# Hymba-style encoder step: order of the first loads, PSUM banks and engine of the token preparation, and the place of the per-layer input transposes

## Chip, core and metric

The kernel runs on one core of one Trainium2 chip, as one program. The metric is the device time of one execution in microseconds (us). A profile of one execution goes with it; its span runs from the first to the last instruction on the core.

## The reference

One layer of a streaming encoder is applied to 2048 prompt tokens and 32 sample tokens of width 1024, all in float32. The part that matters here, shortened:

```python
a  = rmsnorm(x, g_attn)                        # token preparation
z  = a @ w_in                                  # 3072 columns
qa, ka, va, qb, kb, vb = split(z)              # group A: 4 heads, group B: 8 heads
oa = diff_attn(qa, ka, va, t5_bias, lam)       # group A, all earlier keys
ob = band_attn(qb, kb, vb, clip_bias)          # group B, a band of 9 chunks of 64
h  = x + concat(norm(oa), norm(ob)) @ w_out
h  = h + square(relu(rmsnorm(h, g_mlp) @ w_up)) @ w_down
h  = h + sigmoid(h @ w_ple_gate) * (p @ w_ple_proj)   # p: per-layer inputs, 256 wide
y  = rmsnorm(h, g_final)
```

The sample tokens also attend to a cache of 128 keys and values. New keys and values are outputs too.

## The kernel before

Tokens are handled in four blocks (0 to 3) of 512; block 3 also has the 32 sample tokens. Float32 products are made of three matmuls (`mm3`, L164 to L170): each operand is split into a high part in float32r and a low part, and high x high, high x low and low x high are summed in a PSUM bank. `split` (L146) makes the two parts: the high one with a copy on ScalarE (ACT) or VectorE (DVE), the low one with a subtraction on GpSimd (POOL) or VectorE.

The stages that the change touches or displaces, in the order of the source:

1. `consts` (L191) makes the identity and loads four norm weights (`g_attn_s`, `g_mlp_s`, `g_b_s`, `g_sub_s`).
2. `prep` (L297) for blocks 0 and 1: each tile of 128 tokens is loaded (`x`), its mean square is taken on ScalarE (L306), it is transposed on TensorE (PE; `rp`, `xp`), scaled by VectorE (L323) into `a32`, and split into `aH` (VectorE) and `aL` (GpSimd). The transposes use the three banks of the pool `ps_s`.
3. `proj` (L336), group A, blocks 0 and 1: v (`vps`), q and k (`qps`), written to scratch in DRAM (`vS`, `qS`, `kS`). The high and low parts of q and k go through two buffers each, tags `qh` and `ql`.
4. `lam`, `biases` (L227) and `prep_p` (L753). `prep_p` loads the per-layer inputs (`pn`, two buffers), transposes them on TensorE into the pool `ps_t` (`ppt`, tag `tp`, two banks), makes a high part on ScalarE (`pph`, L773) and a low part on VectorE (`ppl`, L774) in the buffers `qh` and `ql`, and stores them in DRAM (`pS`), from where `gate` reads them much later.
5. Attention of group A for queries 0 to 1023 (`attn_a`, matmuls `s`, `tpp`, `o`).
6. Group B projections of blocks 0 to 2, with `prep` of blocks 2 and 3 woven in.
7. Attention of group B for queries 0 to 1023 (`attn_b`, 8 heads with 4 pairs of query tiles each). Per pair: scores `sb` (L704) into `ps_s`, bias and maximum on VectorE (L707), exponential and scaling on ScalarE (L712, L714), transposes `tpb` (L719) into `ps_t` (tag `tp`, the same two banks as `ppt`), high part on ScalarE (`pHb`, L728), low part on VectorE (`pLb`, L729), output `ob` (L744), sum of its halves (L749, L750).
8. `caches` (L446), which transposes the key caches and uses the buffers `qh` and `ql` too; then the group B projection of block 3, the rest of group B's attention, and the group A projections of blocks 2 and 3.
9. Output projection, MLP (`ups`, `dps`) and gate of blocks 0 and 1 around the rest of group A's attention, and then the same for blocks 2 and 3 without attention.

The framework's scheduler, not the source, fixes the order of instructions on each engine: it goes by priorities that follow the source's order, by its own estimate of durations, and by the availability of tile buffers. Buffers of a tag are handed out among its tiles one after another. So projections of a later stage are laid between the attention's instructions on TensorE where the buffers allow it. On each engine, instructions then run in the order written. All loads and stores are issued by SyncE (SP), in order.

Of the kernel before, what the change touches and what calls it, by code (L numbers as in the profile page):

```python
# [44 lines left out]
def toks(b):  # L45
    out = []
    for i in range(4):
        out.append((i * P, P))
    if b == 3:
        out.append((512, SS))  # L50
    return out
# [30 lines left out]
def drain(gen):  # L82
    for _ in gen:
        pass
# [48 lines left out]
class Kern:  # L133
# [57 lines left out]
    def consts(self, cp):  # L191
        nc, a = self.nc, self.a
        self.ident = cp.tile([P, P], F32, name="ident")
        make_identity(nc, self.ident)
        ones = cp.tile([P, P], F32, name="ones")
        nc.gpsimd.memset(ones, 1.0)
        self.ones = cp.tile([P, P], F32R, name="ones_r")
        nc.vector.tensor_copy(self.ones, ones)

        def cols(name, ap, k):  # L200
            t = cp.tile([P, k], F32, name=name)
            self.dma(t, ap.rearrange("(k p) -> p k", p=P))
            return t

        self.g_attn = cols("g_attn_s", a["g_attn"][0], 8)
        self.g_mlp = cols("g_mlp_s", a["g_mlp"][0], 8)
        self.g_b = cols("g_b_s", a["out_norm_b"][0], 4)
        self.g_sub = cols("g_sub_s", a["subln_g"][0], 1)
        nc.vector.tensor_scalar(self.g_sub, self.g_sub, 1.0 - LAM_INIT, None, op0=ALU.mult)
# [84 lines left out]
    def actpair(self):  # L294
        return [self.act.tile([P, 8, BLK], F32R, tag="act", name=n) for n in ("aH", "aL")]

    def prep(self, b, acts, pp, mm, tag):  # L297
        nc = self.nc
        aH, aL = acts[b]
        for c0, n in toks(b):  # L300
            t0 = 512 * b + c0
            x = pp.tile([P, D], F32, tag="x", name="x")
            self.dma(x[:n], self.xsrc(t0, n))
            a32 = pp.tile([P, 8, P], F32, tag="a32", name="a32")
            st = pp.tile([P, 1], F32, tag="st", name="st")
            nc.scalar.activation(  # L306
                a32[:n].rearrange("p a b -> p (a b)"), x[:n], AF.Square, accum_out=st[:n]
            )
            r = self.rsqrt(pp, st[:n], 1, 1.0 / D, EPS, nc.vector, "r1", n)
            rp = mm.tile([P, 512], F32, tag=tag, name="rp")  # L310
            nc.tensor.transpose(rp[:, :n], r.broadcast_to([n, P]), self.ident[:n, :n])
            rb = pp.tile([P, P], F32, tag="rb", name="rb")
            nc.scalar.activation(rb[:, :n], rp[:, :n], AF.Copy)
            xt = pp.tile([P, 8, P], F32, tag="xt", name="xt")
            for h in range(2):
                xp = mm.tile([P, 4, P], F32, tag=tag, name="xp")
                for k in range(4):
                    kk = 4 * h + k
                    nc.tensor.transpose(xp[:, k, :n], x[:n, kk * P : kk * P + P], self.ident[:n, :n])
                nc.scalar.activation(xt[:, 4 * h : 4 * h + 4, :n], xp[:, :, :n], AF.Copy)  # L320
                for k in range(4):
                    kk = 4 * h + k
                    nc.vector.scalar_tensor_tensor(  # L323
                        a32[:, kk, :n], xp[:, k, :n], self.g_attn[:, kk : kk + 1], rb[:, :n],
                        op0=ALU.mult, op1=ALU.mult,
                    )
            self.dma(self.xT[:, :, t0 : t0 + n], xt[:, :, :n])
            self.split(aH[:, :, c0 : c0 + n], aL[:, :, c0 : c0 + n], a32[:, :, :n], "dve", "pool")
            yield

    def ktok(self, b):
# [742 lines left out]
    def run(self):  # L1074
        tc, nc, a = self.tc, self.nc, self.a
        with ExitStack() as top:

            def opened(stack, name, bufs, space=None, side="left"):
                kw = {} if space is None else {"space": space}
                return stack.enter_context(  # L1080
                    tc.tile_pool(name=name, bufs=bufs, side=side, reuse_waits="tile", **kw)
                )

            nc.scalar.preload_act_table_set("natural_log_exp_and_others")
            cp = opened(top, "cp", 1)
            self.dp = opened(top, "dp", 1, bass.MemoryType.DRAM)
            self.wp = opened(top, "wp", 3)
            mm = opened(top, "mm", MM, PSUM)
            tp = mm
            psx = ExitStack()  # L1090
            ps_s = opened(psx, "pss", 5 - MM, PSUM, "right")
            ps_t = opened(psx, "pst", 2, PSUM, "right")
# [4 lines left out]
            sg = opened(s12, "sg", 2)  # L1097
            self.consts(cp)
            with ExitStack() as x:
                pp = opened(x, "pp0", 3, side="right")  # L1100
                acts = {b: self.actpair() for b in HALVES[0]}
                for b in HALVES[0]:
                    drain(self.prep(b, acts, pp, ps_s, "s"))
            ppx = ExitStack()
            pp = opened(ppx, "pp", 1)
            drain(self.proj(HALVES[0], 0, acts, sg, mm, Rings((ps_t, "tp"))))
            with ExitStack() as x:
                wk = opened(x, "setup", 1, side="right")
                self.lam(cp, wk)
                self.biases(wk, ps_t)  # L1110
                self.prep_p(sg, wk, ps_t)
            self.small = True
            mark = tc.tile_snap_priority()
            with ExitStack() as x:
                pool = opened(x, "a0", 1, side="right")
# [19 lines left out]
            weave(self.proj((2,), 1, acts, sg, mm, tp), lifted(self.prep(3, acts, pp, mm, "mm")), 3)  # L1135
            ppx.close()
            self.caches(sg, tp)
            drain(self.proj((3,), 1, acts, sg, mm, tp))
            wqx = ExitStack()
            wq = opened(wqx, "wq", 1, side="right")  # L1140
# [17 lines left out]
            with ExitStack() as x:  # L1158
                pool = opened(x, "a1", 1, side="right")
                for js in JA1:  # L1160
                    self.attn_a(js, pool, ps_s, ps_t, ps_o)
            wk = opened(sq_, "wk", 1)
# [41 lines left out]
            wk = opened(top, "wk4", 1)  # L1204
# [3 lines left out]
            act = Sized(opened(top, "acth", 4), BLK, True)  # L1208
# [75 lines left out]
```

## Time and profile before

| | |
|---|---|
| median of 3 runs | 3315.77 us (3314.72 to 3323.53) |
| the profiled execution | 3310.69 us |
| its span | 3308.8 us |
| granted TensorE clock, mean | 0.975 |
| DVE / ACT / POOL busy | 50% / 51% / 44% |

The page's second part cuts the span into 40 slices. TensorE is busy 90% or more of most of them, with 60% in the first, 80% and more in the third, fourth and some later ones. TensorE busy time is the union of its matmuls, whose ends are modelled, so a share of 90% has little left in it. Times in the views of the trace count from the start of the span.

### The profile page before, as it was taken

To read this page: it belongs to the slowest core of one execution; us is meant where nothing else is said; L and a number is where in the kernel's file an instruction comes from. 1 tells how busy PE (TensorE), PEld (TensorE's weight loads), DVE (VectorE), ACT (ScalarE), POOL (GpSimd) and SP (SyncE) were. 2 spreads that over 40 slices of the span, in tenths; PEclk is the share of its full clock that TensorE was granted. 3 is DMA by queue.
4 is the path that set the end of the run, shared out by engine and by line. 5 is a ranking of instruction groups with operands and counts; after the bars stand their busy time and mean duration, and the time that the engine had idled before them with its cause. 6 is when DMAs were issued, how large, how long until landed. Compare 5 with 4: busy or idle time off the path is not lost. (4 is left out here: it accounts for less than half of the span.)

```text
span 3308.8 us, 50118 instructions
## 1 busy us (share of the span) xinstructions
PE 3096.1 (94%) x17881; PEld 2710.5 (82%) x17881; DVE 1669.4 (50%) x3952; ACT 1698.4 (51%) x3717; POOL 1468.8 (44%) x1083
## 2 busy tenths in 40 slices
PE   6988989999989999999899999989889999999998
PEld 6877778889977888777777877877779999999987
DVE  6117777454555545476765656656442232223335
ACT  4226666566665766666665656654442222222245
POOL 4335654432334433444544444565753333333365
PEclk9999899999999999999999999999999999999999
DMA  7488777686788654545655345347631111111123
GB/s 232 159 252 244 205 217 205 204 247 195 215 235 215 180 145 134 155 132 138 200 136 136 112 132 144 116 146 226 178 105 52 45 46 50 46 45 45 53 86 101
DMA packets 519073, 488.93 MB, mean 148 GB/s; under 512 B 37884, under 2 KB 414016, under 8 KB 518824
## 3 DMA queue, kind: packets, MB, share of 16 engines
q1 hardware_dynamic: 518824, 485.73, 50.8%
q8 instruction: 142, 2.33, 0.3%
q14 instruction: 107, 0.88, 0.1%
HBM read 379.06 MB, written 110.49 MB: 148 GB/s over the span
## 5 line engine op out<-in xcount | busy, mean ns | idle before, releaser
L153 POOL TENSOR_TENSOR wl<-wr,wh 128x1024 fp32r<-128x1024 f32 x338 | 820.0, 2427 | 1026.3 <-ACT wh L149 983.4
L949 DVE TENSOR_TENSOR h<-h,dps 128x512 f32<-128x512 f32 (+1 forms) x640 | 373.1, 585 | 584.6 <-PE dps L170 572.2
L149 ACT ACTIVATE wh<-wr 128x1024 fp32r<-128x1024 f32 x338 | 356.9, 1056 | 563.9 <-PE dps L169 278.4
L168 PE MATMUL dps<-uh,wh 128*128 128x512 f32 (+1 forms) x1280 | 459.7, 359 | 22.0 <-DVE h L949 16.7
L168 PE MATMUL ups<-cH,wh 128*128 128x512 f32 (+1 forms) x1280 | 452.0, 353 | 8.2 <-ACT relu L914 8.0
L170 PE MATMUL dps<-uh,wl 128*128 128x512 f32 (+1 forms) x1280 | 451.7, 353 | 0.0
L169 PE MATMUL ups<-cL,wh 128*128 128x512 f32 (+1 forms) x1280 | 451.5, 353 | 0.0
L169 PE MATMUL dps<-ul,wh 128*128 128x512 f32 (+1 forms) x1280 | 451.4, 353 | 0.0
L170 PE MATMUL ups<-cH,wl 128*128 128x512 f32 (+1 forms) x1280 | 451.0, 352 | 0.0
L168 PEld LDWEIGHTS dps<-uh,wh 128*128 128x128 f32 x1280 | 242.8, 190 | 57.0 <-DVE h L949 22.8
L168 PEld LDWEIGHTS ups<-cH,wh 128*128 128x128 f32 x1280 | 241.4, 189 | 40.9 <-ACT relu L914 8.6
L170 PEld LDWEIGHTS dps<-uh,wl 128*128 128x128 f32 x1280 | 241.7, 189 | 33.0
L169 PEld LDWEIGHTS ups<-cL,wh 128*128 128x128 f32 x1280 | 241.9, 189 | 31.1 <-DVE cL L153 0.4
L170 PEld LDWEIGHTS ups<-cH,wl 128*128 128x128 f32 x1280 | 241.7, 189 | 30.1
L153 POOL TENSOR_TENSOR ul<-relu,uh 128x272 fp32r<-128x272 f32 (+1 forms) x160 | 174.9, 1093 | 205.2 <-ACT uh L149 203.8
L169 PEld LDWEIGHTS dps<-ul,wh 128*128 128x128 f32 x1280 | 242.4, 189 | 26.3
L168 PE MATMUL qps<-aH,wh 128*128 128x512 f32 (+1 forms) x640 | 231.5, 362 | 6.8 <-ACT wh L149 3.4
L545 PE MATMUL s<-ka,q 128*128 128x256 f32 (+4 forms) x784 | 192.7, 348 | 40.8 <-issue 15.7
L169 PE MATMUL qps<-aL,wh 128*128 128x512 f32 (+1 forms) x640 | 229.8, 359 | 0.0
L170 PE MATMUL qps<-aH,wl 128*128 128x512 f32 (+1 forms) x640 | 229.3, 358 | 0.0
L559 ACT ACTIVATE e<-s,nm 128x512 f32<-128x512 f32 (+3 forms) x256 | 155.1, 610 | 94.7 <-DVE nm L551 70.9
L545 PEld LDWEIGHTS s<-ka,q 128*128 128x128 f32 (+1 forms) x784 | 135.7, 195 | 66.4 <-issue 27.9
(217 smaller groups left out, 7056.9 us busy)
## 6 DMA issues: line engine op xcount, KB each, us to landing
wr<-w_up SPq DMA_DIRECT2D x96, 512.0 KB, 4.2
wr<-w_down SPq DMA_DIRECT2D x96, 512.0 KB, 3.7
wr<-w_in SPq DMA_DIRECT2D x74, 512.0 KB, 5.2
q<-qS SPq DMA_DIRECT2D x256, 128.0 KB, 4.3
v<-vSa SPq DMA_DIRECT2D x64, 512.0 KB, 3.8
ka<-kS SPq DMA_DIRECT2D x32, 512.0 KB, 7.9
wr<-w_out SPq DMA_DIRECT2D x32, 512.0 KB, 5.0
wr<-w_ple_gate SPq DMA_DIRECT2D x32, 512.0 KB, 4.4
```

The costliest lines, as they stand in the source:

```text
L149: nc.scalar.activation(hi, raw, AF.Copy)
L153: eng.tensor_tensor(lo, raw, hi.bitcast(F32), op=ALU.subtract)
L168: nc.tensor.matmul(ps, lh, rh, start=start and i == 0, stop=False)
L169: nc.tensor.matmul(ps, lh, rl, start=False, stop=False)
L170: nc.tensor.matmul(ps, ll, rh, start=False, stop=stop and i == n - 1)
L545: nc.tensor.matmul(s, q[:, m, hl, P * qi : P * qi + nr], kt[:, m, k0 : k0 + n], start=hl == 0, stop=hl == 1)
L559: nc.scalar.activation(dst, src, AF.Exp, bias=nmx, accum_out=z[:nr, m, bi : bi + 1])
L949: nc.vector.tensor_tensor(hv, hv, ps, op=ALU.add)
```

## The change

The four norm weights are loaded by a new method `gains`, which `prep` calls once, behind its first token tile's load; the transposes of `prep` for blocks 0 and 1 take banks of `ps_s` (three) and `ps_t` (two) in turn; `aH` is made by ScalarE in every `prep`; and `prep_p` moves from the setup, ahead of group A's first attention, to behind `caches`, with a pool of its own for `pn`.

```diff
@@ consts @@
         nc.vector.tensor_copy(self.ones, ones)
+
+    def gains(self, cp):
+        nc, a = self.nc, self.a
 
         def cols(name, ap, k):
...
-    def prep(self, b, acts, pp, mm, tag):
+    def prep(self, b, acts, pp, mm, tag, first=None):
...
             self.dma(x[:n], self.xsrc(t0, n))
+            if first is not None:
+                first()
+                first = None
...
-            self.split(aH[:, :, c0 : c0 + n], aL[:, :, c0 : c0 + n], a32[:, :, :n], "dve", "pool")
+            self.split(aH[:, :, c0 : c0 + n], aL[:, :, c0 : c0 + n], a32[:, :, :n], "act", "pool")
...
                 for b in HALVES[0]:
-                    drain(self.prep(b, acts, pp, ps_s, "s"))
+                    ring = Rings((ps_s, "s"), (ps_t, "tp"))
+                    drain(self.prep(b, acts, pp, ring, "s", (lambda: self.gains(cp)) if b == 0 else None))
...
                 self.lam(cp, wk)
                 self.biases(wk, ps_t)
-                self.prep_p(sg, wk, ps_t)
...
             self.caches(sg, tp)
+            with ExitStack() as x:
+                self.prep_p(sg, opened(x, "pn", 1), ps_t)
             drain(self.proj((3,), 1, acts, sg, mm, tp))
```

`Rings` hands out the tiles of several pools in turn; `first` runs once.

## The prediction

> **What bounds the kernel now.** I read the page's first part, then the busy time by stage, then the attention of group B by instruction, then the waits around the old place of `prep_p`.
>
> ```profile
> span 3308.8 us, 50118 instructions
> PE 3096.1 (94%) x17881; PEld 2710.5 (82%) x17881; DVE 1669.4 (50%) x3952; ACT 1698.4 (51%) x3717; POOL 1468.8 (44%) x1083
> ```
>
> TensorE sets the end: 212.7 us of the span are all that it idles. A change that leaves its work alone, as this one does (17,878 matmuls before and after, 34 of them moved), can only add or remove idle time, or change its clock. By stage (columns: window, its length, busy PE, PEld, DVE, ACT, POOL, then granted clock, DMA share, GB/s):
>
> ```profile
> 0.00:20.00 20.00, 3.45 (x15) 3.11 (x16) 8.61 (x23) 10.00 (x24) 5.59 (x9) 1.00 0.78 233
> 20.00:60.00 40.00, 32.61 (x237) 30.41 (x236) 37.81 (x95) 20.89 (x56) 25.64 (x15) 0.96 0.76 234
> 210.00:220.00 10.00, 3.10 (x21) 2.93 (x20) 1.38 (x2) 1.19 (x2) 0.00 (x0) 0.71 1.05 350
> 220.00:230.00 10.00, 8.23 (x25) 6.19 (x24) 2.70 (x6) 3.86 (x6) 6.64 (x5) 0.61 0.98 310
> 260.00:500.00 240.00, 203.35 (x1218) 179.73 (x1217) 185.70 (x533) 155.83 (x453) 144.21 (x130) 0.91 0.79 219
> 640.00:922.00 282.00, 268.65 (x1921) 252.14 (x1919) 145.85 (x503) 184.21 (x404) 84.18 (x90) 0.97 0.77 222
> 922.00:1400.00 478.00, 453.77 (x2373) 382.29 (x2373) 249.99 (x744) 301.84 (x598) 193.45 (x126) 0.98 0.64 176
> 1400.00:2210.00 810.00, 762.98 (x3874) 638.90 (x3872) 519.57 (x1082) 500.52 (x1161) 386.83 (x287) 0.99 0.49 135
> 2210.00:3308.00 1098.00, 1051.20 (x6347) 943.54 (x6346) 399.66 (x680) 394.43 (x727) 487.05 (x312) 0.98 0.28 87
> ```
>
> TensorE idles 16.6 us in the first 20 us and 7.4 in the next 40, where VectorE is the full engine (37.81 of 40); 8.7 in 210 to 230, where `prep_p` stands; 13 us in 640 to 922, which holds the first half of group B's attention. What keeps TensorE full there is the projections laid between the attention: of its 268.65 us, first the `qps` and then the `vps` matmuls (columns as above, without engines that don't touch the tile):
>
> ```profile
> 640.00:922.00 282.00, 123.61 (x716) 103.53 (x714) 7.18 (x14) 13.19 (x30) 0.97 0.77 222
> 640.00:922.00 282.00, 62.81 (x432) 56.25 (x432) 6.74 (x18) 0.97 0.77 222
> ```
>
> That is 186.4 us for 1148 matmuls, 0.162 each; attention itself has about 82 us.
>
> **The move of `prep_p`, and what it does to the order.** `ppt` shares the two banks of `tp` with the `tpb` transposes of group B's first half, which now comes ahead of it in the source, and `pph`, `ppl` share the two buffers `qh`, `ql` with the q and k projections of block 3, which come behind it. Buffers of a tag go around in turn, so `prep_p` can't start before that half of the attention has ended, and block 3's projections, and all behind them, not before `prep_p`. The built program's order shows it: between the first and the last `sb` of this half TensorE had 1143 projection matmuls (711 `qps`, 432 `vps`) and now has 120; from position 3163 to 3816 it has nothing but `sb`, `tpb` and `ob`, then the 34 `ppt` in one run with one `ob` between, and then `qps` again. The 1023 others run later, beside the second half and after it.
>
> What does the half cost alone? ScalarE has the most work in it:
>
> ```profile
> L712 ACT ACTIVATE eb<-eb,stb 128x640 f32<-128x640 f32 (+4 forms) x61 | 43.9, 719 | 23.2 <-DVE stb L711 23.2
> L714 ACT ACTIVATE eb<-eb,stb 128x640 f32<-128x640 f32 (+4 forms) x61 | 43.5, 720 | 9.1 <-DVE stb L713 9.1
> L728 ACT ACTIVATE pHb<-tpb 128x128 fp32r<-128x128 f32 (+2 forms) x97 | 39.1, 435 | 18.2 <-PE tpb L719 10.5 <-PE ob L744 6.4
> ...
> L749 ACT ACTIVATE t<-ob 64x256 f32<-64x256 f32 x32 | 12.2, 381 | 10.1 <-PE ob L744 7.6 <-DMA wr<-w_in 1.9
> L712 ACT ACTIVATION_READ_ACCUMULATOR eb<-eb,stb 128x1 f32 x61 | 11.5, 188 | 0.0
> ```
>
> Together 150.2 us in 640 to 922: the lower end for its length. The upper end comes from one pair of query tiles, with the durations of eight full pairs (811.6 to 902.6; last, TensorE busy in it, in all and for `qps`):
>
> ```profile
> L712 ACT ACTIVATE eb<-eb,stb 128x640 f32<-128x640 f32 x16 | 13.3, 828 | 13.2 <-DVE stb L711 13.2
> L714 ACT ACTIVATE eb<-eb,stb 128x640 f32<-128x640 f32 x16 | 13.2, 823 | 1.5 <-DVE stb L713 1.5
> L728 ACT ACTIVATE pHb<-tpb 128x512 fp32r<-128x512 f32 x16 | 9.6, 597 | 6.4 <-PE tpb L719 5.9 <-PE ob L744 0.2
> ...
> L728 ACT ACTIVATE pHb<-tpb 128x128 fp32r<-128x128 f32 x16 | 4.4, 272 | 0.0
> ```
> ```profile
> L707 DVE CUSTOM_DVE_ANT_0 eb<-sb,bb 128x320 f32<-128x320 f32 x32 | 14.3, 484 | 12.3 <-PE tpb L719 10.9 <-POOL ql L153 1.4
> L729 DVE TENSOR_TENSOR pLb<-tpb,pHb 128x512 fp32r<-128x512 f32 x15 | 10.2, 682 | 0.1
> ...
> L750 DVE TENSOR_TENSOR t<-ob,t 64x256 f32<-64x256 f32 x8 | 3.3, 414 | 10.9 <-ACT t L749 10.9
> ```
> ```profile
> 811.60:902.60 91.00, 90.52 (x621) 83.70 (x620) 43.86 (x149) 58.27 (x120) 27.38 (x24) 1.00 0.70 202
> 811.60:902.60 91.00, 63.72 (x357) 52.46 (x356) 4.04 (x8) 6.77 (x15) 1.00 0.70 202
> ```
>
> With the read-out (0.19) and `t` (0.38) of the rows before, a pair costs ScalarE 2 x (0.83 + 0.19 + 0.82 + 0.60 + 0.27) + 0.38 = 5.8 us, and TensorE (90.52 - 63.72) / 8 = 3.35. One tile's chain from score to output is 2 x 0.48 + 0.83 + 0.82 + 0.60 + 0.68 + 0.38 + 0.41 = 4.7 us off TensorE; with the pair's 3.35 on it nowhere hidden, 8.0. `pHb` and `pLb` have one buffer, so a pair's first copy waits for the `ob` of the pair before, and ScalarE, in order, puts the next pair's exponentials into that chain: neither end is reached. I take the middle, 7.0 a pair, a factor of 1.2 on ScalarE's work: the half lasts 150.2 x 1.2 = 181 us (150 to 150.2 x 8.0 / 5.8 = 207). The 1023 matmuls then need 1023 x 0.162 = 166 us elsewhere, in stages where TensorE is 94 to 96% busy (the rows from 922 on), so on the path. Sum 181 + 166 = 347 against 282: **65 us lost** (34 to 91).
>
> **The run of `ppt`** is a chain, with the rows of `prep_p` where it stood:
>
> ```profile
> L773 ACT ACTIVATE pph<-ppt x10: 188/594/602, 195.5 to 238.8; 128x512 fp32r<-128x512 f32 x8, 128x32 fp32r<-128x32 f32 x2
> ...
> DMA to landing us min/median/max: 4.1/6.0/8.2
> ```
>
> Eight pairs of high and low part use two buffers each, so every second one waits until the store two before has landed: 0.59 (copy) + 0.46 (issue, from the three loads in 1.38 us shown below) + 4.1 to 6.0 (landing) = 5.2 to 7.1 us a round. The last `ppt` waits three rounds, 15 to 21 us, in which TensorE has about 3 us of work, and ScalarE, VectorE and TensorE all stand in order behind it: the next head's `tpb` and the two banks of `qps`, whose evacuation needs `qh`. **17 us lost** (12 to 20), a cold start of the clock in it.
>
> **What the old place gives back.**
>
> ```profile
> 218.50 1.94 PE L770 MATMUL ppt<-ident,pn 128*128 128x128 f32 x8 [6.90 <-DMA pn<-p_prompt]
> ```
>
> The 6.9 us before this row are part of the 8.7 us that TensorE idles in 210 to 230. Of its 11.3 us of work there, at a granted clock of 0.71 and 0.61, about a third is the slower clock: some 3 us more. But the new order starts group A's attention at position 1070 instead of 1200, with its first 26 matmuls without a projection between, behind the same stores of bias rows. Gain 0 to 12; I take **4**.
>
> **The start.**
>
> ```profile
> 0.74 0.47 SPq L144 DMA_DIRECT2D g_attn_s<-g_attn  x1
> ...
> 3.05 1.38 SPq L144 DMA_DIRECT2D x<-x_prompt  x3
> ...
> 7.21 1.06 ACT L306 ACTIVATE a<-x 128x1024 f32<-128x1024 f32 x1 [5.19 <-DMA x<-x_prompt]
> ```
> ```profile
> L151 DVE CAST aH<-a 128x1024 fp32r<-128x1024 f32 x8 | 5.5, 689 | 0.2
> ```
>
> The first tile's load goes out 2.3 us sooner. VectorE loses eight casts, 5.5 us of its 37.81 in 20 to 60, and ScalarE, busy 20.89 of 40, takes them at about 1.05 (its L306 row, the same 128x1024). More banks can remove only waits inside the 7.4 us that TensorE idles there. At a DMA share of 0.76 loads may bind next: gain 0 to 2.3 + 7.4 = 9.7; I take 2.3 and half of 5.5, **5 us**. In blocks 2 and 3, nine tiles move 6 us off VectorE and 9.5 onto ScalarE; in 260 to 500 neither is full (185.70 and 155.83 of 240), so I take zero; without that cover it could be 6 won or 9.5 lost.
>
> **Sum.** 3310.69 + 65 + 17 - 4 - 5 = 3383.7 for an execution like the profiled one; the median of the runs lies 5.1 above it, so **3389 us**.
>
> **Rivals.** *ScalarE's pace:* the pairs overlap fully, the half lasts 150 us, and the loss there is 34: 3358. For it: VectorE and TensorE have less to do than ScalarE. Against: one buffer of `pHb`. *A colder clock:* in 260 to 500 TensorE idles 15% and is granted 0.91. Alone with the attention it idles 1 - 82/181 = 55%; in proportion the clock falls by 0.32 to 0.68, a pair's 3.35 becomes 4.9, the pair 8.6, the half 222 us: 41 more, 3430. The Trainium skill, "TensorE: Matmul & The Clock Gate", section "Part 1: The HAM clock gate", says that the clock halves only after an idle window of about 3.4 us; by that rule the short gaps of a pair would leave it full and this rival would be void, and the sum stays 3389. *The other side, holes filled later:* the 1023 matmuls fall into idle time that exists anyway. From 922 to 2210 TensorE idles 24 + 47 = 71 us; if the projections fill these holes, the 65 come back, and if the next head's scores also cover the `ppt` chain, 9 us of gain are left: 3307. It decides from the point where these holes are lack of work; against it, `ups` and `dps` stand ready there all the time, so the holes are waits in order, and no row shows a lack of work. If the chain isn't covered: 3324. *No gain from the start,* because the DMA queues bind: 5 more, 3394.
>
> **Chances.** Forecast, with the start's variant, 0.72; ScalarE's pace 0.12; colder clock 0.08; holes filled 0.05 faster and 0.03 uncovered, no change. A difference under 0.3% (10 us) can't be told from none. So faster 0.05, same 0.03, slower 0.92. The range takes in ScalarE's pace with the other gains at their best, 34 + 12 - 12 - 9.7 = 24, 3340, and the colder clock with the start at zero, 3435.
>
> **What would show it.** After: a stretch of 150 to 220 us with `sb`, `tpb` and `ob` alone and TensorE near half busy, ScalarE the fullest; then some 18 us with hardly anything but `ppt`, `pph` and stores; no wait of `ppt` near 210; the first L306 near 5 us. Wrong would be: projections found inside that stretch, pairs at 5.8 us or less, or TensorE's idle time from there to 2210 smaller by as much as the stretch adds.

## The result and the profile after

| | before | changed |
|---|---|---|
| median of 4 runs each | 3315.24 us (3311.64 to 3323.53) | 3418.21 us (3409.99 to 3428.28) |
| ratio | | 1.0313, 95% interval 1.0282 to 1.0345 |
| the profiled execution | 3310.69 us | 3428.28 us |

The change costs 103 us, where the forecast had 73. The profiled execution after is the slowest of its four, so the two traces differ by more than the medians: 117.7 us of span.

The first lines of the page after:

```profile
span 3426.5 us, 50139 instructions
PE 3156.1 (92%) x17881; PEld 2741.0 (80%) x17881; DVE 1670.0 (49%) x3935; ACT 1719.7 (50%) x3734; POOL 1464.5 (43%) x1083
```

TensorE has the same 17881 matmuls as before (the prediction's 17,878 is 3 short). Its idle time grew from 212.7 to 270.4 us (+57.7), its busy time by 60.0. To see where, both traces were cut at the same events: 60 us, the first score matmul of group A, the first `sb` of group B, the last `ob` of its first half, (after: the end of the `ppt` run,) the first score matmul `s` of group A's second half, its last output matmul `o`, and the end. The columns are as in the prediction: window, length, busy PE, PEld, DVE, ACT, POOL, granted clock, DMA share, GB/s. Before:

```profile
0.00:60.00 60.00, 36.06 (x250) 33.53 (x251) 46.42 (x117) 30.90 (x80) 31.22 (x24) 0.97 0.77 234
60.00:249.70 189.70, 177.18 (x957) 149.62 (x956) 34.31 (x55) 44.49 (x73) 70.99 (x48) 0.96 0.66 208
249.70:620.60 370.90, 327.10 (x2025) 292.15 (x2024) 263.81 (x732) 228.48 (x641) 210.63 (x193) 0.93 0.75 213
620.60:910.90 290.30, 279.79 (x2032) 263.86 (x2030) 148.83 (x522) 190.33 (x427) 86.42 (x94) 0.98 0.76 222
910.90:1364.20 453.30, 430.36 (x2268) 363.25 (x2267) 233.53 (x717) 285.51 (x559) 177.80 (x120) 0.98 0.65 176
1364.20:2193.70 829.50, 779.04 (x3947) 652.91 (x3947) 536.55 (x1126) 515.37 (x1197) 389.61 (x279) 0.99 0.50 139
2193.70:3308.80 1115.10, 1066.57 (x6413) 955.13 (x6412) 405.90 (x687) 403.29 (x744) 502.10 (x329) 0.98 0.28 87
```

After:

```profile
0.00:60.00 60.00, 35.95 (x243) 33.43 (x244) 41.09 (x108) 37.87 (x88) 30.91 (x24) 0.97 0.74 229
60.00:217.40 157.40, 145.41 (x834) 124.34 (x832) 26.14 (x39) 33.23 (x55) 54.65 (x38) 0.99 0.58 183
217.40:588.00 370.60, 324.11 (x1889) 281.12 (x1890) 262.40 (x719) 231.38 (x642) 210.37 (x191) 0.93 0.76 213
588.00:803.00 215.00, 167.63 (x856) 139.94 (x857) 113.62 (x471) 148.70 (x342) 22.13 (x47) 0.76 0.61 170
803.00:828.00 25.00, 7.99 (x40) 5.48 (x40) 6.20 (x13) 7.29 (x15) 1.27 (x1) 0.65 0.89 301
828.00:1314.10 486.10, 464.86 (x2997) 419.66 (x2995) 232.03 (x720) 285.16 (x584) 172.17 (x135) 0.98 0.69 199
1314.10:2142.60 828.50, 786.45 (x3966) 656.85 (x3966) 536.43 (x1121) 514.64 (x1189) 383.96 (x275) 0.98 0.49 138
2142.60:3426.50 1283.90, 1223.72 (x7066) 1080.14 (x7065) 452.05 (x747) 461.46 (x820) 589.04 (x375) 0.98 0.28 88
```

Two rows stand out: the half of group B's attention (588 to 803) idles 47.4 us of TensorE where it idled 10.5 before, at a granted clock of 0.76 in place of 0.98; and the `ppt` run (803 to 828) idles 17.0 at 0.65. These two hold 53.9 of the 57.7 us of added idle time. The half holds most of the added busy time too, for the same matmuls take longer in it. The `sb` matmuls alone, before and after (without the engines that don't touch them):

```profile
620.60:910.90 290.30, 47.17 (x210) 33.04 (x210) 47.03 (x102) 0.98 0.76 222
588.00:803.00 215.00, 63.54 (x210) 39.90 (x210) 46.99 (x102) 0.76 0.61 170
```

Together with `tpb` and `ob`, each tile counted by itself, that is 132.4 us before and 177.5 after, some 45 of the 60.0 us. The attention ends 51 us earlier (2142.6 against 2193.7), but the last row is 169 us longer: the projections that no longer stand between the attention's instructions push other work back, and 653 more matmuls stand at the end, with no attention left to run beside. A reader who looked at the attention alone would take the change for a gain.

The run of `ppt`, by the view of the tile `pph` (what it waits for, who waits for it, then its stores from issue to landing):

```profile
L779 ACT ACTIVATE pph<-ppt x10: 191/597/598, 803.8 to 826.7; 128x512 fp32r<-128x512 f32 x8, 128x32 fp32r<-128x32 f32 x2
...
  DMA pS<-pph: 13.4, 4
...
  PE ppt L776: 15.8, 7
...
DMA to landing us min/median/max: 2.7/4.4/8.0
```

Four copies wait 13.4 us for stores to land, and TensorE's transposes stand 15.8 us behind them.

### The profile page after: what moved, and what is told of

It is laid out like the page before. It is cut to its first block, busy times and chain, and to the rows that moved or that the text cites. A ratio compares the mean times of both kernels' runs of the same rounds, so it can differ in the third digit from the quotient of the medians.

```text
span 3426.5 us, 50139 instructions
## 1 busy us (share of the span) xinstructions
PE 3156.1 (92%) x17881; PEld 2741.0 (80%) x17881; DVE 1670.0 (49%) x3935; ACT 1719.7 (50%) x3734; POOL 1464.5 (43%) x1083
## 4 chain that ended last, share of the span: by engine, by line
PE 51%; DVE 4%; DMA 4%; ACT 2%; issue 1%; POOL 1%; SPq 0%; DVEq 0%; POOLq 0%; ACTq 0%
PE ups L168 6%; PE ups L169 6%; PE ups L170 6%; PE dps L168 6%; PE dps L170 6%; PE dps L169 6%; PE s L551 2%; PE gps L168 2%; PE gps L169 2%; PE gps L170 2%; PE tpp L623 1%; DMA wr<-w_up 1%; PE o L638 1%; PE o L639 1%; DVE e L588 1%
## 5 line engine op out<-in xcount | busy, mean ns | idle before, releaser
L551 PE MATMUL s<-ka,q 128*128 128x256 f32 (+4 forms) x784 | 193.3, 352 | 50.5 <-DMA q<-qS 15.8
```

What stands on the lines that cost most here:

```text
L551: nc.tensor.matmul(s, q[:, m, hl, P * qi : P * qi + nr], kt[:, m, k0 : k0 + n], start=hl == 0, stop=hl == 1)
```

## The experiments

Two questions: which part of the change costs the time, and by what. Batches were run beside the kernel before on one chip each (medians 3307.4, 3314.28 and 3309.25 us).

**Each part alone.** `e1_start_only` is the changed kernel with `prep_p` back at its old place:

```diff
                 self.biases(wk, ps_t)
+                self.prep_p(sg, wk, ps_t)
...
-            with ExitStack() as x:
-                self.prep_p(sg, opened(x, "pn", 1), ps_t)
```

> The changed kernel with the input transposes back in the setup: only the earlier first load, the five banks and ScalarE's aH are left. Theory A (the move of the transposes makes the loss, by holding the projections behind them): the first half of group B's attention is filled again (1160 projection matmuls in it), the time is that of before less the start's gain, 3305 to 3316 us. Theory B (ScalarE's aH or the shared banks make the loss): some tens of us slower than before, 3340 or more. Theory C (the chain of the transposes itself makes it, wherever it stands): as A here.

`e2_move_only` is the kernel before with this move alone.

> The kernel before with the input transposes moved next to the caches, nothing else. Theory A: the whole loss, and the start's gain missing: 3410 to 3430 us, with a stretch of about 160 us without projections. Theory B: within 20 us of before. Theory C: slower by the chain alone, 20 to 30 us: 3335 to 3345.

Measured: the start alone 3319.23 us, ratio 1.0033 (1.0019 to 1.0046); the move alone 3416.08 us, 1.0328 (1.0310 to 1.0347). So the whole loss is the move's. The start was expected to gain and lost a little, which opened a second question.

**What holds the projections.** `e3_own_hilo` leaves the move and gives `pph` and `ppl` buffers of their own:

```diff
-                hi = sg.tile([P, BLK], F32R, tag="qh", bufs=2, name="pph")
-                lo = sg.tile([P, BLK], F32R, tag="ql", bufs=2, name="ppl")
+                hi = wk.tile([P, BLK], F32R, tag="ph", bufs=2, name="pph")
+                lo = wk.tile([P, BLK], F32R, tag="pl", bufs=2, name="ppl")
```

> The changed kernel, but the transposed inputs' high and low parts get two buffers each of their own instead of those of q and k. The transposes still share their two banks with the attention. Theory A: block 3's projections no longer stand behind the transposes, the attention is filled again (1008 projection matmuls in its first half), and the loss goes: 3300 to 3325 us. Theory C: the chain is still there, 3335 or more. If it is the banks and not the high and low buffers that hold the projections: 3400 or more.

`e4_mm_banks` leaves the buffers and takes the banks of `ppt` from the projections' pool instead:

```diff
-                    tp = ps.tile([P, 512], F32, tag="tp", name="ppt")
+                    tp = ps.tile([P, 512], F32, tag="mm", name="ppt")
...
-                self.prep_p(sg, opened(x, "pn", 1), ps_t)
+                self.prep_p(sg, opened(x, "pn", 1), mm)
```

> The changed kernel, but the input transposes use the two banks of the projections instead of the two that the attention's transposes use; the high and low buffers stay those of q and k. Theory A: the transposes no longer wait for the attention's first half, stand ahead of it with projections between them, and the loss goes: 3295 to 3320 us. Theory C: the chain of stores stalls TensorE where it now stands, 3330 to 3345. If the buffers of q and k alone made the loss: 3400.

Measured: 3325.29 us, 1.0051 (1.0031 to 1.0070), and 3334.78 us, 1.0082 (1.0064 to 1.0099). Cutting either link of the chain (banks shared with `tpb` ahead, buffers shared with the projections behind) brings the projections back: 1008 and 1130 of them stand in the half again, of 1143 before. The half in the windows of `e3_own_hilo`:

```profile
587.20:852.00 264.80, 253.55 (x1878) 240.28 (x1879) 138.32 (x513) 177.92 (x403) 71.32 (x85) 0.96 0.75 215
```

11.3 us idle, clock 0.96. The 3334.78 us of `e4_mm_banks` miss theory A's 3295 to 3320 and lie in theory C's 3330 to 3345: with free banks and shared buffers the chain of `ppt` only moves: in `e4_mm_banks` it runs from 567.3 to 605.7, and the stage of group A's first attention, into which it falls, idles 64.8 us against 46.5:

```profile
217.50:589.70 372.20, 307.37 (x1745) 262.00 (x1745) 261.78 (x718) 229.72 (x639) 200.53 (x184) 0.92 0.76 214
```

`e8_move_own_hilo` is the kernel before with the move and the buffers of `e3_own_hilo`, so the counterpart to `e2_move_only`:

> The kernel before with the input transposes moved next to the caches and with high and low buffers of their own, and nothing of the start. Theory A: the projections aren't held, the first half of group B's attention is filled (1130 projection matmuls), and the time is that of before within 15 us: 3300 to 3322. If the move costs something beside the held projections, 3330 or more.

Measured: 3325.36 us, 1.0035 (1.0020 to 1.0050), between the two ranges. Against 1.0328 this one tag pair is worth 0.0293, some 97 us; the new place by itself costs a third of a per cent.

**The clock in the half.** `e5_warm` puts three extra score matmuls ahead of each group of `sb` in the first half; the next `start` overwrites their sum, so the output is unchanged:

```diff
                 s = ps_s.tile([P, 512], F32, tag="s", name="sb")[:nr, :w]
+                if j is not None and j < 4:
+                    for _ in range(3):
+                        c = k0 - kb + w * i
+                        nc.tensor.matmul(
+                            s, q[:, 0, 0, P * qi : P * qi + nr], kt[:, c : c + w], start=True, stop=True
+                        )
```

> The changed kernel with three extra matmuls into each score bank of group B's first half, ahead of the real ones, whose start overwrites them: work for TensorE, nothing for the other engines. It is some 0.15 us a matmul, 12 in a full pair, 1.8 us. Theory W (in the stretch without projections the slow TensorE clock sets the pace): the granted clock there rises from 0.76 towards 1, a full pair takes 7.0 to 7.8 us instead of the 8.5 of the changed kernel, and the kernel is 10 to 30 us faster than the changed one, 3380 to 3410. Theory V (the pace is the chain through ScalarE and VectorE, the clock follows from it and costs nothing): the extra matmuls add to the chain, 8.5 us a pair or more, 3415 to 3445.

`e11_warm_light` has one in place of three.

> The changed kernel with one extra scores matmul ahead of each group of sb in the first half of group B's attention (its sum is overwritten; three were put there in the run e5_warm). If the granted clock sets the pace of the pairs (theory W), the matmuls of ob come 0.12 us apart in most pairs and these pairs follow one another at about 7.0 us; where ob comes 0.21 apart, at 8.5 to 9. Then the stretch is shorter than the changed kernel's 215 us and the kernel 5 to 25 us faster than that one's 3418 if nothing later takes it back. If the pace is the chain through ScalarE and VectorE alone, the pairs stay near 8.4 us whatever the spacing of ob, and the time stays at 3418 to 3430.

Measured: 3446.4 us, 1.0403 (1.0379 to 1.0427), and 3436.02 us, 1.0382 (1.0359 to 1.0406): neither is faster than the changed kernel, against what theory W expected of the time, and both lie a little above the other theory's ranges. The pace of the pairs is another matter. The starts of the first `ob` matmuls of three pairs, in the changed kernel (start, duration):

```profile
724.15 0.42 PE L750 MATMUL ob<-pHb,vbt 128*128 128x256 f32 x1
724.36 0.42 PE L750 MATMUL ob<-pLb,vbt 128*128 128x256 f32 x1
...
732.73 0.41 PE L750 MATMUL ob<-pHb,vbt 128*128 128x256 f32 x1
...
740.00 0.28 PE L750 MATMUL ob<-pHb,vbt 128*128 128x256 f32 x1
```

and of two in `e11_warm_light`:

```profile
734.25 0.28 PE L756 MATMUL ob<-pHb,vbt 128*128 128x256 f32 x1
...
735.00 0.28 PE L756 MATMUL ob<-pHb,vbt 128*128 128x256 f32 x1
735.12 0.28 PE L756 MATMUL ob<-pLb,vbt 128*128 128x256 f32 x1
...
740.64 0.28 PE L756 MATMUL ob<-pHb,vbt 128*128 128x256 f32 x1
```

At a slow clock two `ob` matmuls are 0.21 us apart and the pair takes 8.58 us (724.15 to 732.73); at the full one they are 0.12 apart and a pair takes 6.39 (734.25 to 740.64), four more matmuls included. Over the last 16 pairs, the steps from one slow `ob` group to the next are 8.58 to 9.35 us long in the changed kernel, with one of 11.95 (six steps), and those from one fast group to the next 6.29 to 6.39 in `e11_warm_light` (four); the others change their spacing on the way. The 16 last pairs in the three kernels, changed, three extra, one extra (first and last start of the copy that ends a pair):

```profile
L755 ACT ACTIVATE t<-ob x16: 381/381/382, 677.5 to 804.4; 64x256 f32<-64x256 f32 x16
```
```profile
L761 ACT ACTIVATE t<-ob x16: 380/380/383, 686.3 to 807.4; 64x256 f32<-64x256 f32 x16
```
```profile
L761 ACT ACTIVATE t<-ob x16: 381/381/383, 683.0 to 800.2; 64x256 f32<-64x256 f32 x16
```

That is 15 steps of 8.5, 8.1 and 7.8 us: shorter with the extra matmuls, if not the 7.0 to 7.8 that W expected of `e5_warm`. So the clock is part of the pace. But the half as a whole gained almost nothing, because its earlier pairs took longer with the extra matmuls: it lasts 215.0 us in the changed kernel and 215.0 in `e5_warm`, whose clock there is 0.94. And both kernels lose some 18 to 20 us later, in the second half of group A's attention (here from group B's last `tpb` to the last `s`), where nothing was added; the changed kernel and then `e5_warm`:

```profile
1295.00:2104.00 809.00, 765.90 (x3842) 639.29 (x3842) 519.95 (x1086) 502.33 (x1164) 375.64 (x270) 0.98 0.51 141
```
```profile
591.00:806.00 215.00, 174.37 (x1145) 158.80 (x1145) 113.12 (x471) 150.89 (x343) 22.10 (x47) 0.94 0.62 171
...
1303.40:2130.60 827.20, 773.40 (x3853) 646.10 (x3854) 533.45 (x1088) 503.10 (x1164) 378.01 (x270) 0.97 0.50 138
```

The extra matmuls also changed the order of later work, and this loss is not the clock's (0.97 against 0.98): 10.7 of the 18.2 us are idle time. What the slow clock alone is worth in the kernel's time stays open: these runs can't separate it from the work that they add.

**Why the start gains nothing.** In the trace after, the first transpose starts at 4.55 us and the next tile's `rp` only at 20.61, behind 10.81 us of waiting. TensorE, then VectorE and GpSimd beside it:

```profile
4.55 1.09 PE L325 MATMUL xp<-ident,x 128*128 128x128 f32 x4 [4.55 <-DMA x<-x_prompt]
...
20.61 0.47 PE L317 MATMUL rp<-ident,rsy 128*128 128x128 f32 x1 [10.81 <-DVE rsy L182]
```
```profile
13.63 2.32 DVE L179 TENSOR_TENSOR rsv<-rsv,rsy 128x1 f32<-128x1 f32 x1 [0.58 <-ACT rsy L178]
15.99 2.27 DVE L180 TENSOR_TENSOR rsv<-rsv,rsy 128x1 f32<-128x1 f32 x1
18.29 0.15 DVE L181 TENSOR_SCALAR rsv<-rsv 128x1 f32<-128x1 f32 x1
18.48 2.07 DVE L182 TENSOR_TENSOR rsy<-rsy,rsv 128x1 f32<-128x1 f32 x1
```
```profile
13.59 2.35 POOL L153 TENSOR_TENSOR wl<-wr,wh 128x1024 fp32r<-128x1024 f32 x1 [12.09 <-ACT rsy L178]
15.90 2.34 POOL L153 TENSOR_TENSOR aL<-a,aH 128x1024 fp32r<-128x1024 f32 x1
18.21 2.33 POOL L153 TENSOR_TENSOR wl<-wr,wh 128x1024 fp32r<-128x1024 f32 x1
```

A product of 128x1 has next to nothing to do, and lasts until GpSimd's subtraction ends, three times in a row; the scaling of one input between them takes 0.15. The Trainium skill, "SBUF — State Buffer", section "Who interferes with whom", says that a VectorE instruction with two SBUF inputs contends with a GpSimd instruction that reads SBUF, that the port pair which the two share is an exclusive lock, and that a VectorE instruction with at most one SBUF input, outside its two-port modes, does not contend. The trace agrees: 2.32, 2.27 and 2.07 us with two inputs, 0.15 with one. `e6_before_small_ops` (the kernel before) and `e7_start_small_ops` (`e1_start_only`) write these products with the second factor as a per-partition scalar:

```diff
         nc.scalar.activation(y0, y0, AF.Exp, scale=-0.5)
+        if tag == "r1":
+            eng.tensor_scalar(v, v, y0, y0, op0=ALU.mult, op1=ALU.mult)
+            eng.tensor_scalar(v, v, -0.5, 1.5, op0=ALU.mult, op1=ALU.add)
+            eng.tensor_scalar(y0, y0, v, None, op0=ALU.mult)
+            return y0
```

> The kernel before, with the three products on one value per token in the token preparation written with one tensor input and per-partition scalars instead of two tensor inputs. Theory P (a VectorE instruction with two tensor inputs in SBUF is held while GpSimd subtracts, one with a single tensor input isn't): each takes about 0.15 us also while GpSimd works, TensorE's idle time in the first 60 us falls from 23.9 by 3 to 6 us. The whole is 0 to 8 us faster than before, if the changed order further on doesn't take it back. Rival: these instructions are held all the same, 2.3 us each, and nothing changes at the start.

> The first experiment's kernel (only the earlier first load, five banks and ScalarE's aH) with the same three products in the other form. Theory P: with nothing holding VectorE, the earlier first load now shows: the first projection matmul starts near 17 us instead of 21, TensorE's idle time in the first 60 us falls from 24.9 by 5 to 9 us; 5 to 10 us faster than the first experiment. Rival (the loads bound the start): the first projection still starts at 20 us or later.

Measured: 3314.94 us, 1.0003 (0.9991 to 1.0016), and 3316.29 us, 1.0010 (0.9996 to 1.0023). VectorE in the first of the two, at the place of the waits above:

```profile
12.76 0.27 DVE L180 TENSOR_SCALAR rsv<-rsv,rsy 128x1 f32<-128x1 f32 x1 [0.72 <-ACT rsy L178]
```

The waits are gone: the first `vps` matmul comes at 18.0 us (20.7 before) and at 15.1 (21.2 in `e1_start_only`), and TensorE idles 18.5 and 16.3 us of the first 60 where it idled 23.9 and 24.9. In the kernel before, the 5 us won there are not seen at the end; on top of the changed start the ratio falls from 1.0033 to 1.0010, so that start is no longer slower, and no faster either.

**Both causes taken out.** `e10_mended` is the changed kernel, all four parts of it, with the buffers of `e3_own_hilo` and the products of `e6_before_small_ops`.

> The changed kernel with both suspected causes taken out: own buffers for pph and ppl, and the one-column products of the norm written with a per-partition scalar. The whole of the change's other parts stays. If the two causes are all that the change costs, it is within 0.3% of the kernel before, 3305 to 3325, with projections back in the first half of group B's attention (1130 in the built order), the first vps near 15 to 16 us and TensorE idle by some 16 us in the first 60. If the first ScalarE copies, the five banks or the new place cost something on their own, it stays 0.4% or more slower, 3327 and up.

Measured: 3310.92 us, 1.0003 (0.9991 to 1.0016). The first 60 us and the half:

```profile
0.00:60.00 60.00, 45.07 (x309) 41.48 (x310) 29.97 (x102) 39.97 (x91) 35.81 (x28) 0.97 0.79 243
```
```profile
566.10:847.60 281.50, 271.18 (x2014) 258.43 (x2015) 140.65 (x518) 182.10 (x413) 78.30 (x89) 0.98 0.73 214
```

TensorE idles 14.9 us of the first 60 and 10.3 of the half. The loss is gone, and nothing is won: 9 us more matmul work is done by 60 us than before (45.07 against 36.06), and it does not reach the end. Where it is given back was not followed. None of the ten kernels is faster than the one before by more than its interval.

## Why the prediction came out as it did

**The order: right, and it is the cause.** The prediction read the coupling from the tags: `ppt` behind `tpb` through two banks, block 3's projections behind `pph` and `ppl` through `qh` and `ql`. Cutting either link takes the loss away (1.0328 to 1.0035 for the buffers).

**The half: mechanism right, pair under-sized.** Forecast: 7.0 us a pair, 181 us for the half, 65 lost. Measured: 8.5 us over the last 16 pairs, 215.0 us; with the forecast's own 166 us for the moved matmuls, and the half before taken from its first `sb` to its last `ob`, 215.0 + 166 - 290.3 = 91 us lost. The forecast's window for the half, 640 to 922, left out its first 19 us and took in 11 of the next half; the two slips nearly cancel. ScalarE's work was sized well: the same five lines add up to 46.0 + 44.9 + 39.6 + 12.4 + 11.8 = 154.7 us (150.2 forecast). The factor over it was 215.0 / 154.7 = 1.39, not 1.2. That is at the bound of 8.0 / 5.8 = 1.38, and a full pair, at 8.5 us, is above its 8.0. The bound held only for durations at the full clock, from rows at 1.00. That is the step that failed: the prediction priced a TensorE that it expected half idle with the durations of a full one, and left the clock to a rival. One of its own signs shows it: from 617 to 803 us TensorE does run `sb`, `tpb` and `ob` alone, as forecast, but in the half it is the fullest engine, 167.63 us busy to ScalarE's 148.70, and not near half busy. That rival came nearest here: granted 0.76 (0.68 forecast), pair 8.5 (8.6), half 215 (222). Its whole sum, 3430, was above the 3418 measured, as the main one, 3389, was below.

The rule that the prediction set against this rival (the Trainium skill, "TensorE: Matmul & The Clock Gate", section "Part 1: The HAM clock gate": half speed after an idle window of about 3.4 us) would have left the clock full in short gaps. The trace does not bear that reading out. The waits of TensorE between 588 and 803 (in total, times, longest):

```profile
PE sb L710 <- DVE stb L713: 24.0, 41, 1.0
PE tpb L725 <- DVE pLb L735: 8.6, 4, 4.0
PE sb L710 <- DMA q<-qS: 6.4, 3, 3.4
```

Most are 1.0 us or shorter, only a few reach 3.4 and 4.0, and yet the mean clock over these 215 us is 0.76. One fall can be seen by itself. At 699 us the `ob` matmuls stand 0.12 us apart, and at 706 they stand 0.21 apart; the `sb` groups between them:

```profile
702.12 0.97 PE L710 MATMUL sb<-kbt,q 128*128 128x320 f32 x4 [0.59 <-DVE stb L713]
...
704.73 1.43 PE L710 MATMUL sb<-kbt,q 128*128 128x320 f32 x4 [0.69 <-DVE stb L713]
```

No wait of TensorE from 684 to 705 us is longer than 0.7 us, so this fall needed no long gap. The rival's proportion (15% idle, 0.91) isn't the law either: the half's 22% idle would give 0.87. Nor does any share of idle time alone give the clock, as the half of `e11_warm_light` shows, which idles 22% too, at 0.86:

```profile
586.70:799.00 212.30, 165.42 (x954) 142.14 (x954) 112.34 (x471) 150.15 (x343) 22.06 (x47) 0.86 0.62 172
```

What the runs show is that the clock rises with the matmuls put into the same gaps: 0.76 with none, 0.86 with four more a full pair, 0.94 with twelve. The rule behind it stays open. The rival came near in its sum because it took 55% idle, counting TensorE's work at the full clock's durations.

**The `ppt` run: right.** 17 us forecast; 17.0 us idle in 25.0, the stores' landing as the releaser, and the median of 4.4 us inside the 4.1 to 6.0 used.

**The old place: nothing, not 4.** The hole moved with the start of group A's attention. Before, the windows 210 to 230 idled 8.7 us; after:

```profile
210.00:220.00 10.00, 2.23 (x8) 1.85 (x8) 1.52 (x9) 0.73 (x3) 0.14 (x1) 0.66 0.94 208
220.00:230.00 10.00, 7.86 (x26) 6.63 (x27) 6.38 (x33) 7.35 (x28) 2.29 (x3) 0.50 1.14 260
```

9.9 us, now without any `ppt`: the attention starts with too few projections left to cover its loads (its scores wait 11.1 us for loads of `q`), which the prediction had named as the reason against.

**The start: nothing, not 5.** The first `x` came as early as forecast (the first L312 at 4.4 us, where L306 stood at 7.21), and VectorE lost its casts (41.09 us busy in the first 60, from 46.42). TensorE's idle time there stayed at 24.05 us (23.94 before), because the chain through the 128x1 products sets it, and these were held by GpSimd more often than before: three of 2.1 to 2.3 us in a row instead of two. The prediction looked at how full VectorE was, not at what its shortest instructions waited for.

**Together.** 26 us more in the half and 9 us of gains that did not come make 35. The median lies 29 us above the forecast, the profiled execution 45 above the 3383.7 forecast for one like it; the differences were not taken apart. The other side, holes filled later, is refuted: idle time from the end of the `ppt` run on is 123.5 us, 121.9 before from 910.9 on. Up to the attention's end it fell by 10 us, not by the 54 that the half and the `ppt` run added, and behind it it rose by 12.

## What to carry to other kernels

When a small step is moved, list the buffers and banks that it shares by tag with work before and after its new place: a ring handed out in turn puts everything behind the step in line, and here 34 transposes held back 1023 matmuls. Give such a step its own small buffers first; then its place matters little (1.0035 against 1.0328). And price a stretch in which TensorE will have gaps with rows from a stretch that has them, not from a full one: the clock granted to TensorE belongs to the duration.

## What the hardware showed that was not expected

VectorE's 128x1 product of two SBUF inputs lasts 2.07 to 2.32 us beside a GpSimd subtraction of 2.3 us, and 0.15 to 0.16 once that has ended; with one factor as a per-partition scalar it takes 0.27 beside it. The `ob` matmuls of a pair stand 0.12 or 0.21 us apart, and the spacing changes from pair to pair within 10 us; a fall from one to the other came with no wait over 0.7 us in the 20 us before it. Extra matmuls in the gaps, twelve a full pair, raised the mean clock of the half from 0.76 to 0.94 without making the half shorter.
